# A two-layer encoder trunk on one core: layer 0's prompt FFNs as seven block products, sample's attention beside the prompt's projections

## The chip, the cores and the metric

The kernel runs on one core of one Trainium2 chip. The metric is the device time of one execution in microseconds. Three runs of the kernel before took 3036.11, 3037.09 and 3038.55 us; their median is 3037.09. The engines are TensorE (PE, matmuls into PSUM), VectorE (DVE), ScalarE (ACT), GpSimd (POOL) and SyncE (SP, which issues nearly all DMAs).

## The reference

Two requests go through the same two layers: `x_sample` of 512 tokens and `x_prompt` of 1024, both with 1024 features in float32. Layer 0 mixes tokens with a Fourier transform, layer 1 with grouped-query attention (8 heads of 128, 2 key/value heads, per-head norm, rotary positions). After each mixer comes a SwiGLU FFN of width 2816.

```
x = x + fourier_mixer(x)      # layer 0: real part of a 2-D FFT of rms_norm(x), then @ w
x = x + attention_mixer(x)    # layer 1: softmax(q k^T / sqrt(128)) v, then @ w_o
h = rms_norm(x, g)            # and after either mixer:
x = x + (silu(h @ w_gate) * (h @ w_up)) @ w_down
```

## The kernel before, in words

**Blocks.** Tokens are cut in three blocks of 512: block 0 is sample, blocks 1 and 2 are the prompt. Activations lie transposed, with features on the 128 partitions: a block is 8 chunks of 128 x 512. Residuals are kept in DRAM (`xres`) between stages.

**Precision.** Each operand is split into a high and a low part (`split`, lines 236 to 244: ACT makes the high part, DVE or POOL the low one), and each product is three matmuls (`mm3`, lines 246 to 249). A weight tile of 128 x 1024 is loaded by SP, rounded by ACT (line 278) and subtracted by POOL (line 279).

**The plain FFN** (`ffn`, line 738) runs for one block. For each of 22 chunks of the hidden width it makes gate and up (8 chunks of `h` each, into the two PSUM banks of `bankg`), Silu and product, and then 8 down products, each added by DVE (line 750) to an accumulator. Four accumulator-sized slots (`acc`, half a block each) exist in all, so two blocks can be held; `kept` remembers them, so that the next stage can read a block from SBUF.

**The paired FFN** (`ffn_pair`, line 849) runs for both prompt blocks at once. Gate and up are a product of 2 x 2 blocks: two chunks of the hidden width by two halves of the features, times two halves of the features by two token blocks. It uses seven block products in place of eight, on sums of weights (POOL, lines 924 to 930) and sums of activations. `moving` (line 797) makes the five activation operands that stay in SBUF (`B11`, `B21`, `T2`, `T1`, `B22`) and writes two more to DRAM (`late`), which `moving_late` brings into slot `hA` later. The sums of products are put together by DVE (lines 905 and 915). The down projection stays plain, and its products are taken from the list `pend` between the others (`some`, line 867). Before, only layer 1 uses it.

**Norms.** The last down products of a block, or an output projection, call `new_residual` (line 317): the piece is written to DRAM, squared by ACT (line 329) and summed by DVE (line 330), and at the eighth piece `rstd_cols` sums over partitions on PE (line 299) and takes the reciprocal root by 12 small DVE instructions (lines 287 to 293). `normed` (line 335) spreads the result over the rows on PE (line 308) and makes `h` piece by piece: a multiplication on DVE (348), a rounding on ACT (243), a difference on DVE (244).

**Two streams.** Each stage is a generator that yields its share of work. `weave` (line 1123) runs a main stream "F" and a second one "X", always the one that is less far along in relation to its cost; each has its own pools in SBUF (`sbF`, `sbX`) and in PSUM (`psF`, `psX`; two banks `cF`, two `gF`, two `cX`, one double bank `gX`). The order in which instructions are written sets their priority; the tile framework then arranges each engine's queue ahead of the run, moving up what is ready, except where `pinned` holds it. Slots `hA` and `hB` each hold one block's `h`; `hA` lies in `sbF`, `hB` in `sbX`.

The order of the stages before, main with second stream:

- start-up and sample's Fourier mixer (`lead`, `follow`)
- FFN of layer 0, block 0, with the prompt's Fourier mixer and the norm of block 1
- FFN of layer 0, block 1, with sample's `qkv`, sample's attention and the norm of block 2
- FFN of layer 0, block 2, with sample's output projection, `qkv(1)` and sample's norm
- FFN of layer 1, block 0, with `qkv(2)`, the prompt's attention, both output projections and `moving`
- the pair of layer 1, with nothing beside it

`qkv` (line 993) makes 12 columns of projections of a block: 8 for queries, 2 for keys, 2 for values, each 24 matmuls, with norm and rotation of queries and keys, and writes them to DRAM. `attend` (line 1045) reads them back head by head: scores (PE), maximum (DVE, 1078), Exp (ACT, 1082), scaling (ACT, 1084), transposes (PE, 1096), split (ACT, DVE), values (PE, 1104), copy of the result (ACT, 1107).

## Time and profile before

| what | value |
|---|---|
| median of three runs | 3037.09 us |
| profiled execution, first to last instruction | 3039.1 us |
| PE busy | 2965.8 us, 14184 matmuls |
| DVE, ACT, POOL busy | 1660.7, 1235.4, 1283.2 us |
| matmuls of gate and up, plain FFNs | 4224 |
| matmuls of down products, plain and paired | 3168 |
| DMA | 330.05 MB, mean 109 GB/s |
| mean granted PE clock | 0.995 |

The page states the span alone for the profiled execution; its own whole time isn't listed, so the span stands for it beside the three runs. A line such as `L247 PE MATMUL g<-h,w 128*128 128x512 f32 x1408 | 556.2, 395 | 3.6` reads: line 247, engine, operation, the tile that is written and those that are read, shapes, count; then the busy microseconds of the group, the mean nanoseconds of one, and the idle time of the engine before them with what ended it. Tiles here: `g` and `a` are PSUM banks of gate, up, scores or block products, `c` the banks of down products and projections, `w` weights, `mid` the hidden tile, `pt` transposed probabilities, `acc` an accumulator.

### The profile page before, as it was taken

Reading aid. Unit: us, or ns where it says so; the run is one execution under the profiler, and the core shown is the slowest. Engines: PE = TensorE matmul, PEld = TensorE weight load, DVE = VectorE, ACT = ScalarE, POOL = GpSimd, SP = SyncE. Lnnn points to the kernel's source line nnn. Section 1 sums busy time; section 2 is a strip of 40 time slices with the busy share of each in tenths; the row PEclk is TensorE's granted clock in tenths of the full one; section 3 lists DMA queues with packets and bytes.
Section 4 is the critical chain, followed back from the end, with each engine's and each line's share of the span. In section 5 each row is a group of like instructions: output and inputs, shape, how many; then the busy total and the mean of one; then the engine's idle time right before and its main releaser. Section 6 shows DMA issues by size and latency. Waiting matters only on the chain. (4 is left out here: it accounts for less than half of the span.)

```text
span 3039.1 us, 36901 instructions
## 1 busy us (share of the span) xinstructions
PE 2965.8 (98%) x14184; PEld 2434.2 (80%) x14184; DVE 1660.7 (55%) x2875; ACT 1235.4 (41%) x1843; POOL 1283.2 (42%) x652
## 2 busy tenths in 40 slices
PE   7999999999999999999999999999999999999999
PEld 6778888888877788888878788877787787887777
DVE  6785565534555543533473465665236555655566
ACT  6443232433466522333343577776324222222221
POOL 4434444433333644444433311313636644644452
PEclk9999999999999999999999999999999999999999
DMA  7434543332322734433343211212635411111111
GB/s 228 146 111 149 167 133 93 128 101 84 97 91 94 237 127 133 141 104 101 102 141 108 86 57 53 80 46 91 222 122 183 163 56 55 43 56 56 44 54 63
DMA packets 132080, 330.05 MB, mean 109 GB/s; under 512 B 14176, under 2 KB 28512, under 8 KB 131264
## 3 DMA queue, kind: packets, MB, share of 16 engines
q1 hardware_dynamic: 130688, 318.71, 32.2%
q0 software_dynamic: 928, 7.94, 0.7%
q8 instruction: 111, 1.82, 0.2%
q10 hardware_dynamic: 288, 1.05, 0.1%
q14 instruction: 65, 0.53, 0.1%
HBM read 280.45 MB, written 47.19 MB: 108 GB/s over the span
## 5 line engine op out<-in xcount | busy, mean ns | idle before, releaser
L279 POOL TENSOR_TENSOR w<-raw,w 128x1024 fp32r<-128x1024 f32 x354 | 847.5, 2405 | 1308.2 <-ACT w L278 1225.1
L750 DVE TENSOR_TENSOR acc<-c,acc 128x512 f32<-128x512 f32 x704 | 483.1, 689 | 443.4 <-PE c L249 439.1
L278 ACT CAST w<-raw 128x1024 fp32r<-128x1024 f32 x354 | 371.0, 1049 | 561.7 <-PE c L249 271.7
L247 PE MATMUL g<-h,w 128*128 128x512 f32 x1408 | 556.2, 395 | 3.6 <-ACT t L782 3.6
L249 PE MATMUL g<-h,w 128*128 128x512 f32 x1408 | 552.2, 392 | 0.5 <-POOL w L279 0.5
L248 PE MATMUL g<-h,w 128*128 128x512 f32 x1408 | 552.2, 392 | 0.0
L247 PE MATMUL c<-mid,w 128*128 128x512 f32 x1056 | 417.7, 397 | 15.5 <-DVE acc L750 10.8
L248 PE MATMUL c<-mid,w 128*128 128x512 f32 x1056 | 414.3, 392 | 1.7 <-DVE mid L241 1.7
L249 PE MATMUL c<-mid,w 128*128 128x512 f32 x1056 | 413.6, 392 | 0.0
L241 POOL TENSOR_TENSOR w<-raw,w 128x512 fp32r<-128x512 f32 (+1 forms) x178 | 239.8, 1370 | 310.5 <-ACT w L240 289.5
L863 DVE TENSOR_TENSOR acc<-c,acc 128x512 f32<-128x512 f32 x352 | 240.8, 689 | 186.3 <-PE c L249 185.5
L247 PEld LDWEIGHTS g<-h,w 128*128 128x128 f32 x1408 | 265.3, 188 | 56.7 <-ACT t L782 4.7
L249 PEld LDWEIGHTS g<-h,w 128*128 128x128 f32 x1408 | 265.3, 188 | 56.4 <-POOL w L279 1.6
L248 PEld LDWEIGHTS g<-h,w 128*128 128x128 f32 x1408 | 265.4, 189 | 51.9
L247 PEld LDWEIGHTS c<-mid,w 128*128 128x128 f32 x1056 | 198.2, 188 | 77.5 <-DVE acc L750 20.5
L248 PEld LDWEIGHTS c<-mid,w 128*128 128x128 f32 x1056 | 199.0, 188 | 41.9 <-DVE mid L241 3.7
L249 PEld LDWEIGHTS c<-mid,w 128*128 128x128 f32 x1056 | 198.6, 188 | 40.5
L248 PE MATMUL c<-h,w 128*128 128x512 f32 x480 | 188.2, 392 | 3.0 <-POOL h L241 2.9
L247 PE MATMUL c<-h,w 128*128 128x512 f32 x480 | 189.1, 395 | 0.0
L240 ACT CAST w<-raw 128x512 fp32r<-128x512 f32 (+1 forms) x178 | 107.6, 648 | 196.6 <-PE a L249 79.8
L249 PE MATMUL c<-h,w 128*128 128x512 f32 x480 | 187.0, 390 | 0.0
L1078 DVE TENSOR_REDUCE col<-a 128x1 f32<-128x1024 f32 (+1 forms) x96 | 100.4, 1046 | 127.9 <-PE a L249 127.6
(341 smaller groups left out, 4763.3 us busy)
## 6 DMA issues: line engine op xcount, KB each, us to landing
raw<-in_down_dram SPq DMA_DIRECT2D x110, 512.0 KB, 3.6
raw<-in_gate_dram SPq DMA_DIRECT2D x88, 512.0 KB, 3.5
raw<-in_up_dram SPq DMA_DIRECT2D x88, 512.0 KB, 3.7
raw<-in_qkv_dram SPq DMA_DIRECT2D x36, 512.0 KB, 3.9
t<-xres SPq DMA_DIRECT2D x56, 256.0 KB, 4.0
raw<-in_wo_dram SPq DMA_DIRECT2D x24, 512.0 KB, 3.7
raw<-in_gate_dram SPq DMA_DIRECT2D x44, 256.0 KB, 2.6
raw<-in_up_dram SPq DMA_DIRECT2D x44, 256.0 KB, 3.2
```

The lines of the kernel that those rows point to most:

```text
L240: act.copy(hi, src)
L241: eng.tensor_tensor(lo, src, hi.bitcast(F32), op=ALU.subtract)
L247: pe.matmul(out, lh, rh, start=first, stop=False)
L248: pe.matmul(out, lh, rl, start=False, stop=False)
L249: pe.matmul(out, ll, rh, start=False, stop=last)
L278: pinned(act.copy(flat[:, 0], raw)) if early else act.copy(flat[:, 0], raw)
L279: pool.tensor_tensor(flat[:, 1], raw, flat[:, 0].bitcast(F32), op=ALU.subtract)
L750: dve.tensor_tensor(acc[dc], ps, acc[dc], op=ALU.add)
L863: dve.tensor_tensor(acc, ps, acc, op=ALU.add)
L1078: dve.tensor_reduce(st[:, 0:1], s_in, op=ALU.max, axis=AX.X)
```

## The change

Layer 0's FFNs of blocks 1 and 2 become one paired FFN. Its `moving` runs at the end of the second stream beside the FFN of block 0, in place of the norm of block 1; the pair itself runs with no second stream. At its end the `mT` pool is closed, and `sbX` and `psX` are opened again. Its last down products now go through the norm of a new residual, with the square in a tile of the pool `rT`, and it leaves blocks 1 and 2 in their accumulators (`kept`).

Then a stage of its own follows: main stream sample's `qkv`, attention, output projection and norm; second stream `qkv(1)` and `qkv(2)`. Sample's attention in stream F uses the two `gF` banks for scores and F's three temporary tiles for probabilities, and its rotation table lies in an accumulator slot. Layer 1's FFN of block 0 then has the prompt's attention, the output projections and layer 1's `moving` beside it, without `qkv(2)`. Slots `hA` and `hB` change places in the start-up and the first FFN; three kinds of small column tiles are shared by both streams.

The order after:

- start-up and sample's Fourier mixer
- FFN of layer 0, block 0, with the prompt's Fourier mixer and `moving`
- the pair of layer 0, with nothing beside it
- `qkv(0)`, attention of block 0, its output projection and norm, with `qkv(1)` and `qkv(2)`
- FFN of layer 1, block 0, with the prompt's attention, both output projections and `moving`
- the pair of layer 1

The core of the diff:

```diff
-    def new_residual(b, dc, piece, out=None, stays=False):
+    def new_residual(b, dc, piece, out=None, stays=False, room=None):
...
-            ss[b] = tl("ss", [TB], F32, "ss" + cur[0])
+            ss[b] = room() if room else tl("ss", [TB], F32, "ss" + cur[0])
...
-            sq = bank2()[:, 0]
+            sq = room() if room else side()
...
-            accs[b] = accumulators()
+            accs[b] = kept[b] = accumulators()
+
+        def spare():
+            return tl("sq", [2, TB], F32, "rT", raws)[:, 0]
...
-                new_residual(b, dc, acc, outs[b][:, dc, :])
+                new_residual(b, dc, acc, None if outs is None else outs[b][:, dc, :], room=spare)
...
-        yield from normed(b, g_mix1, got, "BAB"[b], held)
+        yield from normed(b, g_mix1, got, "BAA"[b], held)
...
-        rope = tl("rope", [2, TB], F32, "pX", ap)
+        rope = acc_tile("rope", [2, TB], F32) if cur[0] == "F" else tl("rope", [2, TB], F32, "pX", ap)
...
-                    sc = bank2()
+                    sc = bankg().unsqueeze(1) if cur[0] == "F" else bank2()
...
-                    p = tl("p", [T], F32, "pX", ap)
+                    p = tmp(T) if cur[0] == "F" else tl("p", [T], F32, "pX", ap)
...
-        yield from prepare(1, 0)
...
+        yield from paired(0, None)
+
+    def paired(layer, outs):
...
-        yield from moving((1, 2), g_ffn[1], ops)
+        yield from moving((1, 2), g_ffn[layer], ops)
         close_pool("psX")
-        last["pair"] = ffn_pair(1, (1, 2), ops, t["y"])
+        last["pair"] = ffn_pair(layer, (1, 2), ops, outs)
...
+    weave(ffn(0, 0, lambda: first["h"]), FFN_US, x_0, (80.0 + 60.0) * SLACK + 30.0, 10)
+    weave(last["pair"], 1.0)
+    close_pool("mT")
+    ops.clear()
+    open_pool("sbX")
+    open_pool("psX", **PS)
+    ap = open_pool("ap")
...
+    def main_1():
+        yield from qkv(0)
+        yield from attend((0,))
+        yield from out_projection(0)
+        yield from prepare(0, 1)
+
+    def aux_1():
+        yield from qkv(1, kept[1])
+        yield from qkv(2, kept[2])
+
+    def aux_2():
+        yield from paced(attend((1, 2)), 0.7)
+        for b in (1, 2):
+            yield from paced(out_projection(b), 0.6)
+        close_pool("ap")
+        yield from paired(1, t["y"])
+
+    weave(main_1(), QKV_US + 60.0 + LIN_US, aux_1(), 2 * QKV_US)
+    weave(ffn(1, 0, h_next, t["y"][0]), FFN_US, aux_2(), FFN_US, 9)
     weave(last["pair"], 1.0)
```

More of the change, by code (lines that the diff above doesn't have):

```diff
@@ L210, in col @@
     def col(n):
-        return cols.tile([P, n], F32, tag=f"col{n}{cur[0]}", name=nm("col"))
+        own = "" if n in (2, 3, 4 * NH) else cur[0]
+        return cols.tile([P, n], F32, tag=f"col{n}{own}", name=nm("col"))
     ident = cp.tile([P, P], F32, name="ident")
@@ L376, in load_rows @@
         if seq == "p":
-            x = h_slot("x_p", F32, "A")[:, 0 : 8 * D].rearrange("p (c n) -> p c n", c=8)
+            x = h_slot("x_p", F32, "B")[:, 0 : 8 * D].rearrange("p (c n) -> p c n", c=8)
             xs = [x[:, c] for c in range(8)]
@@ L551, in mixer @@
             ends_folded()
-            u = h_slot("eo", F32R, "A")[:, 0 : 16 * 516].rearrange("p (h k c n) -> p h k c n", h=2, k=2, c=4)
+            u = h_slot("eo", F32R, "B")[:, 0 : 16 * 516].rearrange("p (h k c n) -> p h k c n", h=2, k=2, c=4)
         for j in range(NC // 2):
@@ L673, in mixer_projection @@
             resident[0] = accumulators()
-            first["h"] = h_tile("B")
+            first["h"] = h_tile("A")
         for n in range(NC):
@@ L786, in ffn @@
             pend.extend(lambda dc=dc, m=m, wd=wd, fc=fc: down(m, wd, fc, dc) for dc in range(NC))
-        while pend and layer == 1 and b == 2:
-            one()
     def moving(blocks, gain, ops):
@@ L1155, in trunk_kernel @@
     row_in("s")
-    slot = h_slot("eo", F32R, "A")
+    slot = h_slot("eo", F32R, "B")
     u_s = slot[:, 0 : 16 * 258].rearrange("p (h k c n) -> p h k c n", h=2, k=2, c=4)
@@ L1165, in trunk_kernel @@
     stage = tl("stage", [D], F32, "mid")
-    slot_a = h_slot("wm", F32R, "B")[:, 0 : 16 * TB].rearrange("p (s h k n) -> p s h k n", s=4, h=2, k=2)
+    slot_a = h_slot("wm", F32R, "A")[:, 0 : 16 * TB].rearrange("p (s h k n) -> p s h k n", s=4, h=2, k=2)
     moving_w = [slot_a[:, i] for i in range(4)]
@@ L1202, in prepare @@
     def prepare(b, layer):
-        yield from normed(b, g_ffn[layer], nxt, "B" if b == 2 else "A")
+        yield from normed(b, g_ffn[layer], nxt, "A")
     def h_next():
@@ L1220, in aux_0 @@
         close_pool("mp")
-        yield from prepare(1, 0)
-    x_0 = aux_0()
-    weave(lead(), 1.0)
-    weave(follow(), 1.0)
-    weave(ffn(0, 0, lambda: first["h"]), FFN_US, x_0, (80.0 + 60.0) * SLACK, 10)
-    ap = open_pool("ap")
-    def out_projection(b):
-        got = {}
-        yield from reloaded(dot[b], got, "A" if b == 0 else "B")
-        yield from linear_residual(t["wo"], got["h"], b, xres[b])
-    def paced(stage, f):
-        for v in stage:
-            yield v * f
-    def aux_1():
-        yield from qkv(0, kept[0])
-        yield from attend((0,))
-        yield from prepare(2, 0)
-    def aux_2():
-        yield from out_projection(0)
-        yield from qkv(1)
-        yield from prepare(0, 1)
-    def aux_3():
-        yield from paced(qkv(2, kept[2]), 0.4)
-        yield from paced(attend((1, 2)), 0.65)
-        for b in (1, 2):
-            yield from paced(out_projection(b), 0.5)
-        close_pool("ap")
+        yield from paired(0, None)
+    def paired(layer, outs):
         close_pool("sbX")
@@ L1268, in trunk_kernel, with out_projection, paced @@
     ops = {}
-    weave(ffn(0, 1, h_next), FFN_US, aux_1(), (QKV_US + 60.0) * SLACK, 9)
-    weave(ffn(0, 2, h_next), FFN_US, aux_2(), (LIN_US + QKV_US) * SLACK, 9)
-    weave(ffn(1, 0, h_next, t["y"][0]), FFN_US, aux_3(), FFN_US, 9)
+    x_0 = aux_0()
+    weave(lead(), 1.0)
+    weave(follow(), 1.0)
+    weave(ffn(0, 0, lambda: first["h"]), FFN_US, x_0, (80.0 + 60.0) * SLACK + 30.0, 10)
[5 more added lines that the diff above has]
+    ap = open_pool("ap")
+    def out_projection(b):
+        got = {}
+        yield from reloaded(dot[b], got, "B")
+        yield from linear_residual(t["wo"], got["h"], b, xres[b])
+    def paced(stage, f):
+        for v in stage:
+            yield v * f
+    def main_1():
[14 more added lines that the diff above has]
+    weave(ffn(1, 0, h_next, t["y"][0]), FFN_US, aux_2(), FFN_US, 9)
     weave(last["pair"], 1.0)
```

## The prediction

> **What bounds the kernel now.** I read the engine totals of the page first, then a table of stretches, then the groups of TensorE (PE) instructions inside one stretch, and last the timeline where one stage hands over to the next.
>
> ```profile
> span 3039.1 us, 36901 instructions
> PE 2965.8 (98%) x14184; PEld 2434.2 (80%) x14184; DVE 1660.7 (55%) x2875; ACT 1235.4 (41%) x1843; POOL 1283.2 (42%) x652
> ```
>
> PE is busy 98% of the span and no other engine passes 55%. A matmul's record is longer than its share of PE, though, because the next one starts before it ends:
>
> ```profile
> 2290.07 0.39 PE L247 MATMUL g<-h,w 128*128 128x512 f32 x1
> 2290.29 0.39 PE L248 MATMUL g<-h,w 128*128 128x512 f32 x1
> 2290.52 0.39 PE L249 MATMUL g<-h,w 128*128 128x512 f32 x1
> 2290.75 0.39 PE L247 MATMUL g<-h,w 128*128 128x512 f32 x1
> ```
>
> Each lasts 0.39 us, but the starts lie (2290.75 - 2290.07) / 3 = 0.227 us apart. A matmul that is saved is worth 0.227 us and not 0.39, and a stall is seen as idle only past the first 0.16 us. So PE sets the time nearly everywhere, and the question is what the change takes off PE and where it leaves PE without work. These are stretches of the span (PE, PEld, DVE, ACT, POOL busy us, clock, DMA):
>
> ```profile
> 360.00:550.00 190.00, 187.95 (x873) 156.51 (x871) 111.05 (x199) 60.63 (x79) 79.87 (x34) 0.99 0.40 128
> 543.00:1537.00 994.00, 984.63 (x4581) 810.49 (x4580) 476.78 (x842) 396.16 (x576) 414.57 (x183) 1.00 0.37 119
> 780.00:1010.00 230.00, 223.47 (x1124) 182.30 (x1123) 134.47 (x243) 143.92 (x232) 90.89 (x44) 1.00 0.35 111
> 1700.00:2120.00 420.00, 404.34 (x2345) 339.86 (x2346) 250.85 (x422) 304.27 (x433) 100.10 (x43) 0.99 0.20 64
> 2270.00:2370.00 100.00, 92.25 (x394) 73.09 (x393) 62.17 (x101) 41.76 (x67) 72.16 (x45) 0.98 0.61 206
> 2400.00:3000.00 600.00, 596.97 (x2583) 479.80 (x2583) 349.63 (x529) 154.27 (x254) 317.68 (x198) 1.00 0.15 49
> ```
>
> In order: the end of layer 0's first FFN; the prompt's two layer-0 FFNs with everything beside them; sample's attention inside that; the prompt's attention beside layer 1's first FFN; the hand-over to the block products of layer 1; and those products with nothing beside them. The last is the model for what is new: PE idle 3.03 of 600 us, so neither POOL (53%) nor DVE (58%) holds the seven-product scheme back.
>
> **Part 1: two FFNs become one paired stage.** Two FFNs issue 2 x 22 x 24 x 3 = 3168 matmuls of 512 columns. At 0.227 us that is 719.1 us. The pair issues the same 1056 for the down projection and 7/8 of the 2112 for gate and up, 1848: 2904. In the last row above 2583 matmuls took 600 us, all of them of the pair, so 0.2323 us each, its small stalls included: 2904 x 0.2323 = 674.6 us. **Difference: -44.5 us.** (By pitch alone it would be 264 x 0.227 = 59.9 us; 15 us of it go to the slower beat of the pair.) The bounds of this term are narrow, -42 to -47, since the same code is seen to run.
>
> **Part 2: what ran beside those FFNs now runs by itself.** These are the groups of PE in the second stretch:
>
> ```profile
> L247 PE MATMUL g<-h,w 128*128 128x512 f32 x696 | 274.8, 395 | 0.0
> L247 PE MATMUL c<-mid,w 128*128 128x512 f32 x348 | 136.9, 394 | 2.3 <-DVE acc L750 2.2
> L247 PE MATMUL c<-h,w 128*128 128x512 f32 x256 | 101.6, 397 | 0.0
> L1096 PE MATMUL c<-ident,p 128*128 128x128 f32 x128 | 19.5, 274 | 1.9 <-ACT p L1084 1.9
> L247 PE MATMUL c<-pt,w 128*128 128x256 f32 x64 | 18.7, 293 | 2.7 <-ACT pt L240 2.7
> L247 PE MATMUL a<-w,w 128*128 128x512 f32 x32 | 13.2, 411 | 0.8 <-ACT p L1082 0.8
> ```
>
> Three lines (L247 to L249) make one triple, so the FFNs have 3 x (696 + 348) = 3132 matmuls there, 711 us. The rest of the 994 us, 283 us, is the wall time of sample's and the first prompt block's projections, sample's attention and its output projection. At least 9.4 us of that (994 - 984.63) is idle. The change runs these among themselves, together with the second prompt block's projections, which leave layer 1's first FFN: 12 x 8 x 3 = 288 matmuls, 65 us, added in one place and removed in the other, so nothing net.
>
> Whether 283 us suffice without an FFN as filler is the largest unknown. A bound from below: no idle, -9. From above I look at what attention does to ScalarE (ACT) in the third stretch:
>
> ```profile
> L1082 ACT ACTIVATE p<-a,col,rqc 128x512 f32<-128x512 f32 x32 | 24.9, 779 | 35.2 <-DVE col L1079 34.9
> L1084 ACT ACTIVATE p<-p,col 128x512 f32<-128x512 f32 x32 | 23.2, 724 | 1.5 <-DVE col L1083 1.5
> L240 ACT CAST pt<-c 128x512 fp32r<-128x512 f32 x32 | 18.6, 583 | 3.5 <-PE c L1096 3.4
> L1082 ACT ACT_TABLE_LOAD x9 | 11.5, 1283 | 0.2
> L782 ACT ACT_TABLE_LOAD x9 | 11.5, 1283 | 0.2
> ```
>
> Softmax and its split keep ACT busy for 24.9 + 23.2 + 18.6 = 67 us, while attention's own matmuls are about 96 x 0.227 + 128 x 0.11 + 192 x 0.118 = 58 us of PE (for 128 and 256 columns, estimates in proportion to width with a small fixed part). Projections beside it have the opposite leaning, and the 23 us of table loads fall away, because no Silu alternates with Exp there. PE stands still for 6.5 of 230 us in that stretch and for 15.7 of 420 in the prompt's attention, 3 to 4%. On some 350 us that would be 10 to 14 us, about what is in the 283 already. **I take 0.** For the upper bound, the pace of sample's heads, two copies of a result for each:
>
> ```profile
> L1107 ACT COPY t<-c x16: 347/373/374, 810.5 to 995.0; 128x256 f32<-128x256 f32 x16
> ```
>
> That is (995.0 - 810.5) x 2/15 = 24.6 us for a head, 197 for eight. With that pace kept, 58 us of attention and 65 of projections leave PE 74 us short; covered half by other work, **+37**.
>
> **Part 3: the hand-over into the pair.** `moving`, with its POOL splits and the rows written out to DRAM, now ends beside layer 0's first FFN. In layer 1 that place (2270 to 2370) has 7.75 us of PE idle; the end of layer 0's first FFN as it stands (360 to 550) has 2.05. The waits there:
>
> ```profile
> PE c L247 <- DVE acc L750: 5.6, 4, 2.7
> ```
>
> DVE stands in `moving` for a POOL split to free an input, and the additions of the down products queue behind. 7.75 - 2.05 = 5.7; layer 0 spreads it over more of the FFN. **I take +5**, bounds 0 and 10.
>
> **Part 4: the hand-over out of the pair.** Nothing is beside it, and what follows needs norms. Layer 1's pair ends so on DVE:
>
> ```profile
> 3022.14 0.70 DVE L915 TENSOR_TENSOR a<-a,t 128x512 f32<-128x512 f32 x1
> 3022.75 0.69 DVE L863 TENSOR_TENSOR acc<-c,acc 128x512 f32<-128x512 f32 x1
> 3023.36 0.69 DVE L905 TENSOR_TENSOR a<-a,t 128x512 f32<-128x512 f32 x1
> ...
> 3032.79 1.39 DVE L863 TENSOR_TENSOR acc<-c,acc 128x512 f32<-128x512 f32 x2 [0.35 <-PE c L249]
> 3034.53 1.39 DVE L863 TENSOR_TENSOR acc<-c,acc 128x512 f32<-128x512 f32 x2 [0.35 <-PE c L249]
> ```
>
> Two additions take 1.74 us, and thirteen remain after the last product. In layer 0 each of the last sixteen also gives a Square on ACT and one more addition on DVE, for the norm:
>
> ```profile
> L330 DVE TENSOR_TENSOR ss<-a,ss 128x512 f32<-128x512 f32 x63 | 43.3, 687 | 23.9 <-ACT a L329 23.4
> L348 DVE TENSOR_TENSOR a<-c,t 128x512 f32<-128x512 f32 x32 | 22.2, 692 | 6.0 <-DMA t<-xres 5.8
> L244 DVE SCALAR_TENSOR_TENSOR h<-a,gains,h 128x512 fp32r<-128x512 f32 x48 | 35.9, 748 | 13.0 <-ACT h L243 13.0
> L243 ACT ACTIVATE h<-a,gains 128x512 fp32r<-128x512 f32 x48 | 33.0, 688 | 52.9 <-DVE a L348 52.8
> ```
>
> DVE starts dependent-free work every 0.61 us (3022.14, 3022.75, 3023.36), so a pair of down products costs it 4 x 0.61 = 2.4 us: thirteen take 16 us, after 2 us for the last hidden tile. Sample's projections need only its old residual, so their norm follows at once: 0.69 + 0.69 + 0.75 = 2.1 us to the first piece of `h`. PE has 13 x 3 x 0.227 = 9 us of work in these 20: 11 idle. Then two norms share DVE, and PE gets a piece of `h` every 2.6 us or so for each stream; two columns per stream would fill that, one would fill half. I add 5. **+16**, bounds 8 (the norm gets in between the additions) and 30 (one column at a time).
>
> **Part 5: the norm ahead of layer 1's first FFN** was hidden beside another FFN and now ends the main stream, when the second stream is nearly dry. Its chain: addition 0.69, Square 0.6, addition 0.69, sums on PE, the reciprocal root, the rows, then 2.1 to the first piece. The middle of such a chain runs, from the sums to the spread rows:
>
> ```profile
> 1444.11 0.95 PE L299 MATMUL c<-ones,t 128*128 128x1 f32 x8
> 1445.09 0.17 DVE L287 TENSOR_SCALAR c<-c 128x4 f32<-128x4 f32 x1
> ...
> 1447.93 0.16 DVE L293 SCALAR_TENSOR_TENSOR yk<-c,col 128x4 f32<-128x4 f32 x1
> 1450.73 0.46 PE L308 MATMUL c<-t,ones 128*128 128x128 f32 x2
> ```
>
> 7 us beside other work, so 11 in all. The prompt's attention that follows can fill a little. **+10**, bounds 5 and 16.
>
> The clock granted is 0.98 in the stretch 2270 to 2370, with stalls of at most 2.7 us by the wait above. [...]
>
> **The sum:** -44.5 + 0 + 5 + 16 + 10 = **-13.5 us** on the span of 3039.1. That span lies 2.0 us above the median of the runs, 3037.1, and within 0.6 of the slowest; from the median the forecast is **3023.6 us**.
>
> **The rivals.**
> 1. *The scheduler fills the gaps.* The order within an engine isn't fixed by the weave alone, and the hand-over at 550 shows next to no loss. All the lower bounds: -44.5 - 9 + 0 + 8 + 5 = -40.5, so 2997 us. Against it: in part 4 nothing is there to fill with.
> 2. *The hand-overs cost about double*, +10, +30 and +16 with nothing else wrong: +11.5 at the extreme, around 3037 when two of three do so. The saving is real but is paid out again. For it: DVE is the bound of both ends, and it serves both streams.
> 3. *Attention without cover (slower).* The place is the stage of part 2. Sample's attention shares three temporary tiles and two score banks with the main stream, and the second stream halts in the middle of it until the first prompt block's projections give back the slot of `h` and the next norm is through. With its heads at the pace of part 2 and half of the shortfall covered, +37: 3061. It turns the sign once the stage loses 13.5 us more than it loses now. Against it: the present pace is set by the weave's shares, not by the chain.
> 4. *No saving*: the pair in layer 0 runs slower than in layer 1 because DMA or POOL is short. The row 2400 to 3000 with DMA at 0.15 leaves nothing of it.
>
> **How the numbers follow.** A change within 0.2%, 6 us, can't be told from none. Forecast (-6 to -30): 0.47. Rival 1: 0.13. Rival 2: 0.17, its results on both sides of zero but mostly inside 6 us. Rival 3 and rival 2 at its extreme: 0.22. Rival 4: 0.01. Faster: 0.47 + 0.13 = 0.60; same 0.17; slower 0.23. The likeliest case's own range is 3007 to 3031. For 8 in 10 the range goes down to rival 1's 2997 and up to 3046, where rival 3 is partly in.
>
> **What would show it.** Matmuls: 264 fewer in all. Pair in layer 0: about 430 matmuls per 100 us and PE idle about 0.5. Part 4: one gap of some 10 us of low PE with DVE at 90% or more at the end of that stage, and no other row of the sort before it. Part 2: PE idle at 3 to 4% in the projections' stage and ACT near 90% in its attention; 10% idle there would make rival 3 right. Part 5: a gap of 8 to 12 us ahead of the first `g<-h,w` of layer 1, released by DVE or ACT in the norm. Wrong altogether if the stage of part 2 takes over 385 us (283 + 65 + 37).

## The result and the profile after

The changed kernel took 3072.65 us (median of four runs, 3067.43 to 3078.92), the kernel before 3037.82 beside it: a ratio of 1.0117, 95% interval 1.0099 to 1.0135. It is 35 us slower, where 13.5 us faster was forecast, and it lies outside the range (2997 to 3046). The profiled execution has a span of 3075.5 us against 3039.1, so 36.4 us are to be found. These are two lines of its page and a table of stretches, with the columns of the prediction's table (us; PE, PEld, DVE, ACT, POOL busy; clock, DMA share, GB/s).

```profile
span 3075.5 us, 36702 instructions
PE 2956.2 (96%) x13920; PEld 2405.6 (78%) x13920; DVE 1752.0 (57%) x3037; ACT 1209.5 (39%) x1907; POOL 1344.4 (44%) x762
```

```profile
600.00:1200.00 600.00, 596.83 (x2583) 479.90 (x2583) 346.61 (x524) 153.78 (x253) 312.47 (x196) 1.00 0.15 51
1215.00:1282.00 67.00, 48.48 (x151) 33.40 (x150) 49.84 (x92) 31.53 (x50) 17.45 (x8) 0.72 0.59 200
1282.00:1639.00 357.00, 338.51 (x1715) 276.36 (x1714) 155.95 (x380) 196.79 (x344) 122.11 (x61) 0.98 0.38 117
1639.00:1674.00 35.00, 21.06 (x85) 16.69 (x84) 21.39 (x57) 19.08 (x29) 5.90 (x3) 0.76 0.53 172
```

PE has 264 matmuls fewer, as forecast. The first stretch is the new pair: 2583 matmuls in 600 us, PE idle 3.17, the beat of layer 1's pair to the matmul. The other three are what used to lie beside the FFNs: the hand-over out of the pair, the projections with sample's attention (called the middle below), and the end, up to layer 1's first FFN. In the middle PE is busy for 95% of the time, and none of DVE, ACT and POOL for more than 56%.

PE's busy time flatters such stretches, because one record is longer than its share of PE (0.39 us against 0.227 from start to start) and longer still at half clock (0.63 us against 0.43, in the products from 1237.27 to 1238.98 of the hand-over). So I counted otherwise, from the starts of PE's instructions in the trace: each is given the pitch that it has in steady rows (0.227 us for 512 columns, 0.118 for 256, 0.110 for 128, 0.112 for one column), and what the wall has beyond that is called **lost**. The kernel before lost 141.2 us of its span in this sense, the kernel after 237.7, while the work fell from 2889 to 2829 us. The hand-over starts at the pair's last block product, and the end is always the 35 us that close about 5 us behind the first FFN product of layer 1.

| stage | lost before, us | lost after, us |
|---|---|---|
| start, to 100 us | 27.2 | 35.1 |
| FFN of layer 0, block 0 | 18.5 | 23.0 |
| layer 0, prompt: two FFNs with all beside them / the pair | 21.1 | 16.7 |
| hand-over out of the pair, 66 us | in the row above | 37.8 |
| middle, 357 us | in the row above | 39.8 |
| end, 35 us | in the row above | 20.6 |
| FFN of layer 1, block 0 | 53.9 | 44.8 |
| pair of layer 1 | 20.4 | 20.0 |

The profiled execution took 3077.33 us, 4.7 more than the median. Part of its loss at the start is its own: the start-up lost 29 to 35 us from one profile of the experiments to another. The saved work is 59.9 us; hand-over, middle and end lose 98.2. The timeline shows how, first in the hand-over (start, us, engine, line, operation; in brackets the idle time before and what ended it).

```profile
1220.21 23.73 SPq L324 DMA_DIRECT2D xres<-acc  x14
1222.20 0.50 PE L248 MATMUL c<-mid,w 128*128 128x512 f32 x1 [2.38 <-DVE acc L866]
...
1228.04 1.87 PE L300 MATMUL c<-ones,sq 128*128 128x1 f32 x8 [2.89 <-DVE sq L331]
...
1232.18 0.80 PE L248 MATMUL c<-mid,w 128*128 128x512 f32 x1 [0.79 <-DVE acc L866]
...
1247.11 1.87 PE L300 MATMUL c<-ones,sq 128*128 128x1 f32 x8 [4.91 <-DVE sq L331]
...
1254.60 0.79 PE L248 MATMUL c<-h,w 128*128 128x512 f32 x1 [0.58 <-ACT h L244]
...
1654.97 1.28 ACT L244 ACTIVATE h<-g,gains 128x512 fp32r<-128x512 f32 x2
1656.11 1.40 DVE L245 SCALAR_TENSOR_TENSOR h<-g,gains,h 128x512 fp32r<-128x512 f32 x2
1657.49 0.79 PE L248 MATMUL a<-w,w 128*128 128x512 f32 x1 [3.07 <-ACT p L1085]
...
1666.96 0.68 DVE L242 TENSOR_TENSOR pt<-c,pt 128x512 fp32r<-128x512 f32 x1
1667.79 0.55 PE L248 MATMUL c<-pt,w 128*128 128x256 f32 x1 [5.75 <-ACT h L244]
...
1668.57 0.63 PE L248 MATMUL g<-h,w 128*128 128x512 f32 x1
```

The last block product is at 1215.8, the first projection at 1254.6. PE does the remaining down products, both norms' sums, then the rows of both norms, and only then a projection, in that order, and nearly each step waits for DVE or ACT. At the end the first piece of `h` for layer 1 is whole by 1656.8 (1656.11 plus half of 1.40), but the first FFN product runs at 1668.57: in PE's queue, score products and a values product of the prompt's attention stand ahead of it, the last of which needed `pt` from DVE, done at 1667.64. Not all of these 11.8 us could have been won by another order, since the last piece of that `h` is whole only at 1668.96. So the same DVE and ACT serve two chains in turn, and PE waits for the one that it happens to hold first. These are the waits of the hand-over, the middle and the end, the largest of each (us in total, times, longest):

```profile
PE c L300 <- DVE sq L331: 7.8, 2, 4.9
PE c L248 <- DVE acc L866: 4.5, 5, 2.4
...
PE g L248 <- ACT t L1085: 9.1, 5, 5.2
...
PE a L248 <- ACT p L1085: 7.1, 2, 4.0
PE c L248 <- ACT h L244: 5.7, 1, 5.7
```

### The profile page after: what moved, and what is told of

It is laid out like the page before. It is cut to its first block, busy times and chain, and to the rows that moved or that the text cites. A ratio compares the mean times of both kernels' runs of the same rounds, so it can differ in the third digit from the quotient of the medians.

```text
span 3075.5 us, 36702 instructions
## 1 busy us (share of the span) xinstructions
PE 2956.2 (96%) x13920; PEld 2405.6 (78%) x13920; DVE 1752.0 (57%) x3037; ACT 1209.5 (39%) x1907; POOL 1344.4 (44%) x762
## 4 chain that ended last, share of the span: by engine, by line
PE 81%; DVE 5%; POOL 4%; issue 4%; DMA 3%; ACT 3%; SPq 0%; POOLq 0%; ACTq 0%; DVEq 0%
PE c L248 12%; PE c L249 12%; PE c L250 11%; PE a L248 8%; PE a L250 7%; PE a L249 7%; PE g L248 7%; PE g L250 7%; PE g L249 7%; PE c L1099 2%; POOL w L280 1%; POOL w L242 1%; DVE col L1082 1%; DVE col L1081 1%; DMA x<-xres 1%
## 5 line engine op out<-in xcount | busy, mean ns | idle before, releaser
L280 POOL TENSOR_TENSOR w<-raw,w 128x1024 fp32r<-128x1024 f32 x244 | 583.4, 2397 | 1014.5 <-ACT w L279 941.7
L242 POOL TENSOR_TENSOR w<-raw,w 128x512 fp32r<-128x512 f32 (+1 forms) x332 | 435.3, 1334 | 509.0 <-ACT w L241 485.7
L279 ACT CAST w<-raw 128x1024 fp32r<-128x1024 f32 x244 | 255.6, 1049 | 485.1 <-issue 216.6
L248 PE MATMUL c<-mid,w 128*128 128x512 f32 x1056 | 419.0, 400 | 17.2 <-DVE acc L751 11.3
L241 ACT CAST w<-raw 128x512 fp32r<-128x512 f32 (+1 forms) x332 | 195.5, 635 | 396.9 <-PE a L250 153.3
L248 PE MATMUL g<-h,w 128*128 128x512 f32 x704 | 279.7, 397 | 4.2 <-ACT t L783 4.2
L250 PE MATMUL g<-h,w 128*128 128x512 f32 x704 | 277.1, 394 | 2.2 <-POOL w L280 2.2
L249 PE MATMUL g<-h,w 128*128 128x512 f32 x704 | 277.5, 394 | 0.0
L248 PEld LDWEIGHTS c<-mid,w 128*128 128x128 f32 x1056 | 198.0, 189 | 85.4 <-DVE acc L866 21.3
L250 PEld LDWEIGHTS c<-mid,w 128*128 128x128 f32 x1056 | 199.4, 189 | 41.9
L248 PE MATMUL c<-h,w 128*128 128x512 f32 x480 | 195.6, 409 | 5.8 <-ACT h L244 1.9
L249 PE MATMUL c<-h,w 128*128 128x512 f32 x480 | 194.2, 405 | 7.2 <-POOL h L242 5.2
L250 PE MATMUL c<-h,w 128*128 128x512 f32 x480 | 191.6, 400 | 0.4 <-POOL w L280 0.4
L248 PEld LDWEIGHTS g<-h,w 128*128 128x128 f32 x704 | 133.4, 190 | 31.5 <-ACT t L783 5.6
L250 PEld LDWEIGHTS g<-h,w 128*128 128x128 f32 x704 | 133.4, 189 | 30.6 <-POOL w L280 3.1
L249 PEld LDWEIGHTS g<-h,w 128*128 128x128 f32 x704 | 133.4, 189 | 25.7
L250 PE MATMUL a<-B,w 128*128 128x512 f32 x352 | 138.0, 392 | 3.8 <-POOL w L242 3.8
```

The lines of the kernel that those rows point to most:

```text
L241: act.copy(hi, src)
L242: eng.tensor_tensor(lo, src, hi.bitcast(F32), op=ALU.subtract)
L248: pe.matmul(out, lh, rh, start=first, stop=False)
L249: pe.matmul(out, lh, rl, start=False, stop=False)
L250: pe.matmul(out, ll, rh, start=False, stop=last)
L279: pinned(act.copy(flat[:, 0], raw)) if early else act.copy(flat[:, 0], raw)
```

## The experiments

Each kernel is the changed one but for its edit. Times are medians, beside the kernel before on the same chip. Lost time is given as hand-over / middle / end; the changed kernel has 37.8 / 39.8 / 20.6.

**1. Is it DVE's work for the norms, or the clock?** Theory A: the additions for the two norms, on DVE between those of the down products, set the hand-over. Theory B: the clock granted there is low (0.72, 0.76 in the rows above), and PE is slow rather than starved.

```diff
-        else:
-            sq = room() if room else side()
+        elif room is None:
+            sq = side()
             act.activation(sq, piece, AF.Square)
```

> Edit: the residuals at the end of every paired or plain stage that gives its squares a tile of the pair's pool are no longer squared and summed, except the first piece; the norms of the two prompt blocks rest on that one piece. It leaves out 14 Squares on ACT and 14 additions on DVE in the hand-over out of layer 0's pair (1215 to 1285 us of the changed kernel, where PE idles 19 of 70 us). Theory A, the norm's sums on DVE hold the last down products: 14 x 0.61 = 8.5 us of DVE go, the hand-over gets 8 to 12 us shorter, the time falls from 3072.7 to about 3062. Theory B, the gaps themselves lower the clock and the half-rate matmuls are the price: a shorter gap also means fewer half-rate windows, so 15 to 20 us off. Theory C, sample's attention is the loss: at most 3 us off.

3056.16 us, 1.0061 [1.0044, 1.0077]; lost 23.0 / 40.9 / 22.2. Fourteen Squares and additions are worth 15 us in the hand-over and nothing elsewhere: A accounts for 15 of its 38. The time at half clock there fell with them, from 37.5 to 20.5 us by the clock records of the traces, so these 15 us don't yet tell A from B. The stretch shrinks from 66 to 51 us:

```profile
1213.00:1264.00 51.00, 42.39 (x145) 27.77 (x144) 38.85 (x79) 23.43 (x36) 16.62 (x7) 0.80 0.78 263
```

For B, matmuls without use were put in the gaps:

```diff
             if fc == NF - 1:
+                if outs is None and b == blocks[0]:
+                    busy(30 if dc == NC - 1 else 4)
...
+        if outs is None:
+            busy(16)
...
         yield from out_projection(0)
+        busy(60)
```

> Edit: small 128-column matmuls on constants are added where PE waits: 4 after each of the last eight down products of layer 0's pair, 30 ahead of the last norm there, 16 behind the pair, 60 ahead of sample's norm before layer 1's FFN (some 140 in all, about 15 us of PE at full clock, placed in gaps of 19 and 14 us). Nothing of the computation is left out. Theory B, the lowered clock in and after the gaps is the price: the granted clock in the two hand-overs rises from 0.73 and 0.76 towards 1, and the time falls by 8 to 15 us. Theory A, the chain on DVE and ACT is the price and PE would wait anyway: no gain, or up to 8 us lost to the added matmuls. Theory C: no change, within 4 us.

3079.42 us, 1.0138 [1.0120, 1.0156].

```profile
1210.00:1281.00 71.00, 58.53 (x294) 47.58 (x293) 49.37 (x92) 31.08 (x49) 16.58 (x7) 0.83 0.51 178
1643.00:1678.00 35.00, 25.12 (x167) 21.77 (x168) 18.44 (x49) 14.77 (x24) 1.21 (x1) 0.90 0.43 135
```

The clock rose from 0.72 to 0.83 and from 0.76 to 0.90, and no time came back: from the pair's last block product to the first FFN product took 10.6 us more for 29 us of added matmuls (the trace holds 268, where some 140 were expected). Fillers may also stand in the way of real work, so this alone doesn't decide. The end says it better. From the last output projection to the first FFN product the changed kernel takes 28.1 us, 14.6 of them at half clock; the first kernel of experiment 3 takes 28.1, with 19.1 at half clock. There, 4.5 us more of half clock cost no time that shows. For the hand-over no run changes the clock and leaves the work. A bound can be counted: the products that began at half clock are 14.4 us of work at full pitch in the hand-over, 7.5 in the middle and 6.0 at the end, and at half clock 512 columns took 0.43 us from start to start in place of 0.227, so these products took at most about as much again. So B can be at most 28 of the 98 us lost, and less where the work behind them waited anyway. It isn't the main cause; as a part of the hand-over it isn't excluded.

**2. Is it sample's attention?** It is left out; the output projection reads the residual in its place.

```diff
-        yield from reloaded(dot[b], got, "B")
+        yield from reloaded(xres[b] if b == 0 else dot[b], got, "B")
...
-        yield from attend((0,))
```

> Edit: sample's attention is left out altogether; its output projection reads sample's residual instead of the attention's result. What goes are 58 us of matmuls on PE by pitch, and whatever stalls attention brings to the stage. Theory C, attention without an FFN beside it is the loss: the time falls by 58 plus 30 to 37 us, to about 2980, and the stretch between the pair and layer 1's FFN shows PE idle under 2% outside its two ends. Theories A and B, the loss sits in the hand-overs: the time falls by 58 to 65 us, to about 3010.

3008.29 us, 0.9904 [0.9886, 0.9921]; lost 37.2 / 32.1 / 16.9. That is 64 us less than the changed kernel, of which 58 are attention's own matmuls, as the prediction estimated (the trace has 416 matmuls fewer, 58.5 us by their pitches). By the medians its chain costs some 6 us more than its work; by the count of the profiled executions the three stretches lose 12 less. Neither is the 37 of rival 3. Without it the middle still loses 32, now at the ends of columns in the one stream that is left.

**3. Is it the slot of `h`, the order of the norms, the banks, or a queue?** First the slot that the second prompt block's norm has to wait for (`h_slots`), then sample's norm moved ahead of the last down products (`norm_first`).

```diff
-        yield from normed(b, g_mix1, got, "BAA"[b], held)
+        yield from normed(b, g_mix1, got, "ABA"[b], held)
```

> Edit: one word. Block 0's projections take slot hA, block 1's hB and block 2's hA (in the changed kernel hB, hA, hA), so the second prompt block's norm can be made as soon as sample's projections are through and need not wait for the first prompt block's. Theory C in its narrow form, the second stream halts in the middle of sample's attention for that slot (PE stands 5.4 us at 1413 us and PE idles 13.5 of 100 us there): 5 to 12 us off. Theories A and B: 0 to 3 us off.

3073.00 us, 1.0113 [1.0096, 1.0129]; 35.2 / 40.7 / 21.7. So the second stream's halt costs nothing that shows.

```diff
+        if outs is None:
+            h0.update(norm_first())
         while pend:
```

`norm_first` runs all of `normed(0, g_mix1, got, "A")`.

> Edit: sample's first norm of layer 1 is written ahead of the pair's remaining down products, into slot hA, which the pair's last products set free; the rotation table takes a buffer of the hidden tiles, and the slots are hA, hB, hA as in the run h_slots. Nothing is left out. Theory A2, after the sums on DVE the rest of the hand-over is a queue: loads of sample's residual behind 14 writes on SP, the rows of its norm on PE behind all down products, DVE with both: PE gets projections to do during the tail, the hand-over (66 us for 28 us of work) gets 12 to 22 us shorter, the time falls to about 3055. Theory D, the pace there is DVE's total work, and what goes first only changes the order: less than 6 us off.

3089.71 us, 1.0176 [1.0160, 1.0191]; 35.8 / 55.1 / 15.1. Slower by 17. The rows of the norm and the last down products now shared the two `c` banks, so the first projection still began only at 1261.0, 45 us after the last block product, and the middle lost 15 more.

```profile
1216.00:1281.00 65.00, 41.86 (x154) 30.61 (x153) 43.72 (x85) 29.88 (x48) 14.25 (x7) 0.74 0.56 189
1281.00:1641.00 360.00, 331.72 (x1654) 271.38 (x1653) 166.87 (x386) 194.66 (x341) 120.52 (x60) 0.95 0.37 117
```

Three single suspects of the same kind. The prompt's attention begun before the end:

```diff
         yield from qkv(2, kept[2])
+        for _ in range(8):
+            yield next(later)
...
+    later = attend((1, 2))
...
-        yield from paced(attend((1, 2)), 0.7)
+        yield from paced(later, 0.7)
```

> Edit: the first eight steps of the prompt's attention (keys, values and the first score tiles of its first head) are moved from layer 1's FFN to the end of the second stream, so that they stand beside sample's output projection and norm. Nothing is left out. If the stretch ahead of layer 1's FFN (35 us for 14 us of work) is PE without work, these steps fill 4 to 8 us of it and as much leaves the FFN's stage: 4 to 10 us off. If it is the chain of sample's norm that counts and PE has nothing worth filling with, 0 to 3 us.

3073.16 us, 1.0123 [1.0106, 1.0140]; 37.1 / 38.2 / 19.2. The fourteen writes that hold SP's queue from 1220 to 1244, put on POOL's:

```diff
-            sp.dma_start(xres[b][:, dc, :], piece)
+            (pool if room else sp).dma_start(xres[b][:, dc, :], piece)
```

> Edit: the sixteen writes of the prompt's residual at the end of layer 0's pair are issued from POOL's queue in place of SP's. Nothing is left out. If the loads of sample's residual come late because they stand behind these writes on SP (the first load is issued at 1250 us, the writes from 1216 to 1244), the hand-over gets 3 to 8 us shorter. If the loads are late only because the work ahead of them on PE and DVE is, less than 2 us.

3071.89 us, 1.0117 [1.0102, 1.0132]; 37.0 / 38.9 / 20.0. And other paces for the first stream:

```diff
-        yield from qkv(0)
-        yield from attend((0,))
+        yield from paced(qkv(0), 0.4)
+        yield from paced(attend((0,)), 1.4)
...
-    weave(main_1(), QKV_US + 60.0 + LIN_US, aux_1(), 2 * QKV_US)
+    weave(main_1(), 196.0, aux_1(), 170.0)
```

> Edit: the shares of the two streams in the projections' stage are changed, sample's projections first (weight 0.4), its attention spread wider (weight 1.4), so that attention lies beside the end of the first and all of the second prompt block's projections. Nothing is left out. The run without attention says that attention brings about 6 us of stalls of its own: at most 4 to 6 us off if more cover helps. If the stage's loss is in the ends of its chains (norms of keys, the second prompt block's norm), the same or up to 8 us slower, because the ends come at other places and not fewer.

3075.24 us, 1.0127 [1.0112, 1.0142]; 37.4 / 41.2 / 21.6. None of the three moves the time.

**4. The banks of the hand-over.** Once the block products are done, their banks are free. First the last down products and the sums of the norms take those (`tail_banks`), then sample's norm goes ahead as well, its rows in a `g` bank (`norm_banks`).

```diff
         def down(m, wd, fc, b, dc):
-            ps = bank()
+            ps = tail_bank() if ending else bank()
...
-                new_residual(b, dc, acc, None if outs is None else outs[b][:, dc, :], room=spare)
+                new_residual(b, dc, acc, None if outs is None else outs[b][:, dc, :], room=spare, ps=tail_bank if ending else None)
```

> Edit: the down products that remain after the last product of layer 0's pair, and the sums of both norms there, take PSUM banks of the pair's own pool (four, idle by then) in place of the two banks of the projections. The order of the work is left. Nothing is left out. Theory E, the projections' two PSUM banks are the narrow place of the hand-over: with the order unchanged only the additions' waits go, 3 to 8 us off the changed kernel. Theory A, the sums on DVE are: less than 3 us.

3075.83 us, 1.0124 [1.0106, 1.0143]; 39.2 / 42.7 / 21.6. Nothing.

```diff
+        if outs is None:
+            h0.update(norm_first())
...
+        r = in_rows(rstd[0], ps=bankg())
```

> Edit: as norm_first (sample's norm written ahead of the pair's remaining down products, slots hA, hB, hA), and besides the remaining down products and the sums of both norms take banks of the pair's pool, the rows of sample's norm take a bank of the gate products, and its product with the residual is made in place in SBUF. So both banks of the projections are free while the tail runs. Nothing is left out. Theory E (norm_first gained nothing because the rows held one of two banks and the tail the other, so that no projection could start before 1259 us): projections start within 15 us of the last product, the hand-over gets 15 to 25 us shorter, the time falls to 3048 to 3058. Theory D (DVE's total work sets the pace): within 5 us of the changed kernel.

3076.21 us, 1.0134 [1.0117, 1.0151]; 27.6 / 57.6 / 15.1. The hand-over gives 10 us, and the middle takes 18.

```profile
1209.00:1265.00 56.00, 42.20 (x145) 31.68 (x145) 40.09 (x81) 24.96 (x41) 10.61 (x5) 0.79 0.56 188
1265.00:1628.00 363.00, 334.61 (x1660) 273.25 (x1660) 169.83 (x389) 199.85 (x348) 125.02 (x62) 0.95 0.37 121
```

**5. The end.** Output projection of sample from slot A and more of the second stream kept for the end:

```diff
-        yield from normed(b, g_mix1, got, "BAA"[b], held)
+        yield from normed(b, g_mix1, got, "ABB"[b], held)
...
-        yield from reloaded(dot[b], got, "B")
+        yield from reloaded(dot[b], got, "BA"[b == 0])
...
-    weave(main_1(), QKV_US + 60.0 + LIN_US, aux_1(), 2 * QKV_US)
+    weave(main_1(), 228.0, aux_1(), 160.0)
```

> Edit: sample's projections, output projection and layer-1 norm all use slot hA, both prompt blocks' projections hB, and the second stream gets a smaller share (160 to 228), so that the second prompt block's last columns stand beside sample's norm. Nothing is left out. If the 35 us ahead of layer 1's FFN (14 us of work) are a chain that dense matmuls can cover, 8 to 15 us off. If the second stream only ends later and the same wait comes behind it, under 3 us.

3067.49 us, 1.0100 [1.0084, 1.0115]; 34.2 / 47.1 / 12.3. The end gives 8, the middle takes 7. With the edit of `norm_banks` added (`both`):

> Edit: norm_banks and slots_end together. Nothing is left out. If the two hand-overs are independent and both are PE without work, the gains add: 23 to 40 us off the changed kernel, 3033 to 3050, at best level with the kernel before. If the loss is in what DVE and ACT have to do in this part of the program, at most 8 us.

3075.45 us, 1.0129 [1.0113, 1.0144]; 27.7 / 51.4 / 21.0.

**6. Shared temporaries (rival 3).** Sample's attention gets three buffers of its own for probabilities, in place of the main stream's temporaries; then the same with the edit of `slots_end`.

```diff
-        "wF": 4, "wX": 4, "rawF": 2, "rawX": 2, "tF": 3, "tX": 4, "ssF": 1, "ssX": 2, "pX": 2,
+        "wF": 4, "wX": 4, "rawF": 2, "rawX": 2, "tF": 3, "tX": 4, "ssF": 1, "ssX": 2, "pX": 3,
...
-                    p = tmp(T) if cur[0] == "F" else tl("p", [T], F32, "pX", ap)
+                    p = tl("p", [T], F32, "pX", ap)
```

> Edit: sample's attention takes its probability tiles from the second stream's pool again, which gets three buffers in place of two, so that it does not share the main stream's three temporary tiles. Nothing is left out. If those shared tiles hold attention up (the mechanism named in the slower rival), 8 to 15 us off and PE's loss between 1410 and 1490 us falls from 20 to under 10. If the chain of each tile or its order on ACT and DVE holds it up, under 4 us.

3069.64 us, 1.0108 [1.0092, 1.0125]; 37.2 / 38.3 / 21.4.

> Edit: slots_end and own_temps together. Nothing is left out. slots_end alone gave about 5 us; if buffers matter, 13 to 20 us off the changed kernel, 3053 to 3060; if they don't, the same 5 us as slots_end, 3064 to 3070.

3071.91 us, 1.0105 [1.0083, 1.0127]; 37.8 / 41.9 / 13.7. Neither can be told from its partner without the buffers.

By now one thing was plain: hand-over, middle and end together lost 93 to 106 us in every one of these orders (86 without the norms' sums or without sample's attention). Most of what is taken away in one place comes back in another.

**7. The second half of the change alone.** Layer 0's prompt goes back to two plain FFNs, with only the norms beside them; the projections, sample's attention and its output projection stay by themselves, as in the change.

```diff
+        while pend and layer == 0 and b == 2:
+            one()
...
-        yield from paired(0, None)
+        yield from prepare(1, 0)
...
-    weave(last["pair"], 1.0)
+    weave(ffn(0, 1, h_next), FFN_US, prepare(2, 0), 60.0, 9)
+    weave(ffn(0, 2, h_next), FFN_US)
```

> Edit: the second half of the change without the first, as part_2_alone, and the last eight down products of the prompt's second block are made at the end of their FFN. Nothing is left out. If the pair is worth 44.5 us less its hand-overs' 21 as predicted, about 3096. If the hand-over out of a plain FFN costs as much as that out of the pair (its norm too has to be summed before the prompt's projections), 3110 to 3120, and the pair is worth its full 44 us. If the loss comes from the pair standing in front, 3060 to 3075.

3099.32 us, 1.0204 [1.0189, 1.0219]: 62 us slower than before. An earlier form of this kernel, in which block 2's last eight down products were made inside layer 1's first FFN and block 2's norm there was still the mixer's (it leaves layer 0's FFN out of that norm), had taken about the same time:

> Edit: the second half of the change without the first. Layer 0 keeps three plain FFNs (the two of the prompt now with nothing but a norm beside them), and then comes the changed kernel's stage of projections, sample's attention, output projection and norm, and layer 1 as changed. Nothing is left out. By the prediction's terms the pair is worth 44.5 us and its hand-overs cost 21, so this kernel should be 23 us slower than the changed one, about 3096. If the loss of the stage belongs to the missing FFN cover alone, it shows the same 60 us of lost PE time between the hand-over and layer 1's FFN, and a hand-over of some 10 to 15 us instead of 38, so about 3090. If the loss comes from the pair standing in front, the stage loses 25 to 30 us there and the kernel takes about 3060 to 3070.

3101.32 us, 1.0205 [1.0185, 1.0226]. These are the stretches of the complete form, the one of 3099.32 us: the two FFNs, the hand-over, the middle and the end.

```profile
543.00:1255.00 712.00, 707.75 (x3118) 585.27 (x3117) 317.94 (x482) 191.06 (x241) 306.64 (x130) 1.00 0.34 106
1255.00:1295.00 40.00, 31.69 (x114) 21.73 (x112) 32.11 (x60) 17.37 (x28) 8.27 (x4) 0.83 0.52 171
1295.00:1656.50 361.50, 341.02 (x1735) 279.20 (x1736) 161.97 (x387) 201.23 (x349) 122.79 (x61) 0.98 0.38 117
1656.50:1691.50 35.00, 20.35 (x85) 15.99 (x84) 21.87 (x59) 19.30 (x29) 7.66 (x4) 0.76 0.56 184
```

The two FFNs alone lose 7.4 us in 710; hand-over, middle and end lose 17.8 / 39.8 / 20.7. Together that is 85.7. The kernel before lost 21.1 with this work mixed, but it had the second prompt block's projections beside layer 1's first FFN, which without them loses some 11 us less here. So **the cover of the FFNs was worth about 54 us** by this count; the spans of the two profiled executions differ by 55.3, and the medians by 62. The middle and the end lose what they lose in the changed kernel, with no pair in the program; only the hand-over loses 20 us less. And the changed kernel, with the pair for the two plain FFNs, lies 1.0117 - 1.0204 = -0.0087 from this one, 26 us faster: the first half of the change is a gain by itself.

**8. A better balance.** In experiment 4 the hand-over's gain went into the middle, perhaps because its two streams ended apart. So `norm_banks` with other shares, and the same with the slots of experiment 5 (195 : 160):

```diff
-    weave(main_1(), QKV_US + 60.0 + LIN_US, aux_1(), 2 * QKV_US)
+    weave(main_1(), 150.0, aux_1(), 2 * QKV_US)
```

> Edit: norm_banks with the main stream's share lowered from 172 to 150, so that the prompt's projections keep pace with sample's, whose norm no longer counts. Nothing is left out. If norm_banks lost its 10 us because sample's attention came too early beside the second stream's norm, 8 to 15 us off norm_banks, 3061 to 3068. If what PE loses there is fixed by the chains and only changes its place, within 4 us of norm_banks.

3062.47 us, 1.0082 [1.0066, 1.0099]; 28.6 / 48.4 / 16.2.

```profile
1209.00:1266.00 57.00, 43.32 (x145) 32.54 (x144) 39.95 (x81) 24.94 (x41) 10.59 (x5) 0.73 0.57 186
1266.00:1632.00 366.00, 342.43 (x1718) 279.07 (x1718) 175.89 (x405) 205.14 (x353) 131.52 (x65) 0.97 0.40 125
```

> Edit: both (norm_banks and slots_end) with the main stream's share lowered from 228 to 195. Nothing is left out. If the shares were the reason, the gains of the hand-over (10 us) and of the end (5 us) add: 3055 to 3062. If the loss only changes its place, 3068 to 3078.

3066.22 us, 1.0094 [1.0075, 1.0113]; 25.6 / 43.5 / 22.2. The first kernel of this experiment, `norm_banks` with 150, is the best order found, 10 us below the changed kernel and still 25 above the one before. Against the changed kernel its hand-over loses 9 us less, its end 4 less and its middle 9 more. No version here that does all of the work beats the kernel before.

## Why the prediction was wrong

| term | predicted, us | measured, us | how |
|---|---|---|---|
| part 1, the pair | -44.5 | -43.2 | 59.9 less work, 16.7 lost in it |
| part 2, the rest by itself | 0 | +18.7 | middle 39.8, against 21.1 for the whole stage before |
| part 3, into the pair | +5 | +4.5 | first FFN, 23.0 against 18.5 |
| part 4, out of the pair | +16 | +37.8 | hand-over |
| part 5, norm at the end | +10 | +20.6 | end |
| not in the sum | 0 | -1.6 | start +7.9, FFN of layer 1 -9.1, its pair -0.4 |
| sum | -13.5 | +36.8 | the spans differ by 36.4 |

**Parts 1 and 3 were right.** The beat of the pair could be read from layer 1, and it held in layer 0. In the first FFN, PE's wait for the down products' additions rose from 2.0 to 5.0 us between 360 and 550, as part 3 has it. The changed kernel is 26 us faster than experiment 7's, near the -23.5 to which the prediction's parts 1, 3 and 4 sum, but that nearness is partly luck: experiment 7's kernel has a hand-over of its own, with 17.8 us lost, which the sum doesn't hold.

**The step that failed is the price of taking the cover away: "I take 0" in part 2, and the sizes of parts 4 and 5.** For these three the prediction has 0 + 16 + 10 = 26 us; they measured 18.7 + 37.8 + 20.6 = 77.1. The difference of 51 us is as large as the whole error of the forecast (36.8 + 13.5). In part 2 I read PE idle for 3 to 4% in the stretches of attention and called that "about what is in the 283 already". Those rows were taken with an FFN beside them, whose independent matmuls filled nearly every wait for a maximum, an exponential or a norm. They show what attention costs with cover and say nothing on what it costs without. By itself +18.7 lies inside the bound of +37 that I gave for part 2, and the 9.1 us that layer 1's FFN loses less may be set against it, since the second prompt block's projections left that stage. What was far off is the three together, and experiment 7 measures them without the pair: 62 us. In the middle PE is idle for 5.2% by the row (18.5 of 357), but 11% is lost by the starts. My own sign for rival 3, 10% idle, would have missed it, since busy time hides waits under 0.16 us (0.39 - 0.227) and the stretches at half clock, 17.1 us there. The other sign, over 385 us for the stage, stood at its limit: from the first projection at 1254.6 to the last at 1640.5 it took 386.

**Parts 4 and 5 had the right mechanism and half the size.** The gap in the hand-over has DVE at 49.84 of 67 us, not "90% or more". Of 37.8 us, 15 go with the norms' additions (experiment 1). A hand-over out of a plain FFN, with the sums of one norm in its tail in place of two, loses 17.8 (experiment 7); the two figures overlap and don't add up to an account of the 37.8. I had counted 13 down products for DVE with their sums (15 remained), and 11 us for the norm at the end, where the way from the last output projection to the first FFN product took 28.1. I had not counted that the order of PE's queue is laid down ahead of the run, and what stood behind a waiting instruction there waited too: the rows of the first norm, three of whose four inputs ACT had made by 1220.0, ran from 1248.84, behind the sums of the second; and at the end the first FFN product ran behind a values product, 11.8 us after the first piece of its `h`. Where the first norm went ahead into banks of its own (experiment 4), the first projection began 11 us after the last block product in place of 39, and the hand-over lost 10 us less.

**The rivals.** Rival 3 had the sign and came within 12 us of the time (3061), but most of its mechanism is refuted: own buffers and another slot change next to nothing (experiments 3 and 6), and leaving attention out takes away only 6 to 12 us beyond its work. Its two score banks are another matter. Of the middle's 18.5 us of idle PE, 9.1 are score products that wait for a bank which an Exp has still to free (`PE g L248 <- ACT t L1085`), 9.6 in experiment 7's kernel; no run gave attention more score banks. Rival 2's doubled ends came true in kind, 37.8 + 20.6 against its 30 + 16, but its extreme ended at +11.5, as it had nothing for part 2. Rival 1 is the reverse of what happened, and rival 4 is out by the pair's row. The forecast has no term for the clock. The granted clock fell to half for 37.5 us in the hand-over and for 17.1 each in the middle and the end (means 0.72, 0.98 and 0.76 in the rows above). What that cost is bounded in experiment 1 and not measured.

**What stays open.** Of the middle's 40 us I can name the waits for score banks (9.1 us, the longest 5.2, behind the first Exp) but not one cause. Experiments 3 to 8 show that the three losses trade against each other; that they are one shortage of independent work is the reading that fits all runs, and it is argued, not shown run by run. That the missing cover costs this much, pair or no pair, is shown by experiment 7.

## What to carry to other kernels

Before work is moved out from beside a dense stage, price the dense stage as cover: the idle share of a mixed stretch is the price with cover, and the price without it has to be bounded from chain lengths, as wall time of the dependent work over its PE work. One run that makes only the uncovering half of a change (here experiment 7) separates a saving from its bill at once. And count stalls from start to start against the pitch, as busy time hid half of them here (51 of the 98 us show as idle PE).

## What the runs showed of the hardware

**Additions on DVE beside subtractions on POOL.** The change moved the Square's result from PSUM to SBUF (`room=spare`), so that the addition L331 has two inputs in SBUF. Beside a weight subtraction on POOL such an addition took 2.41 us, the next one 0.69:

```profile
1243.37 2.35 POOL L280 TENSOR_TENSOR w<-raw,w 128x1024 fp32r<-128x1024 f32 x1 [23.57 <-ACT w L279]
1243.85 2.41 DVE L331 TENSOR_TENSOR sq<-sq,sq 128x512 f32<-128x512 f32 x1 [0.27 <-ACT sq L330]
1246.37 0.69 DVE L331 TENSOR_TENSOR sq<-sq,sq 128x512 f32<-128x512 f32 x1
```

Its form before, with one input in PSUM (`ss<-a,ss`), lasts at most 0.694 us in 63 instances, 45 of which ran beside a subtraction on POOL in whole or in part. In attention a product of two single columns took up to 2.377 us; this is sample's, in the kernel before (min/median/max in ns):

```profile
L1079 DVE TENSOR_TENSOR col<-col,nrqc x32: 150/160/2377, 797.6 to 988.4; 128x1 f32<-128x1 f32 x32
```

Twelve of those 32 last over 0.4 us and take 17.2 of their 20.4 us, and an Exp stands behind each. Each of the twelve ran beside a subtraction on POOL and ended within 0.03 us of its end. In the hand-over two of the fourteen additions with both inputs in SBUF met a subtraction; they ended 0.56 and 0.54 us behind its end and took (1.63 - 0.68) + (2.41 - 0.68) = 2.7 us more than two of median length. That the subtractions held them is read from these times; no run here took the subtractions away.

**Half clock.** In the clock records of the two kernels' traces the granted clock is full or half; the records at half last 3.4, 6.8, 13.7 or 23.9 us (at the end of the execution 3.6 and 3.7), 116 us in all after the change against some 31 before (the mean clocks 0.981 and 0.995 give the same). At the end of the projections' stage 4.5 us more of it cost no time that shows (experiment 1); for the hand-over only a bound is known. At the start the two went together: in the first 100 us the kernel before has a mean clock of 0.93 and lost 27.2 us, the changed kernel 0.86 and 35.1, and from one profile of the experiments to another the same instructions ran 13.7 to 23.9 us at half clock and lost 29 to 35 us; part of the 11.5 us between the changed kernel's fastest and slowest run may lie there.
